# Pair 13 of the second layer's last down product: seven products instead of eight

## The chip, the cores and the metric

The kernel runs on one core of a Trainium2 chip. The time is the device time of one execution in microseconds (us); the figure for a kernel is the median of its runs. The core has a matrix engine (TensorE; PE in the profile, PEld for its weight loads), a vector engine (DVE), a scalar engine (ACT), GpSimd (POOL) and SyncE (SP), whose queue issues the loads of the weights. Each engine works through its own instructions in a fixed order and waits for the others by semaphores. Matmuls accumulate in PSUM, in eight banks of 128 x 512 floats; everything else lies in SBUF.

## The reference

Two layers over 256 tokens of width 2048. The first layer mixes tokens by a convolution module, the second by multi-head latent attention; behind each mixer stands an MLP with a squared ReLU, of inner width 8192, and a final norm ends it all. The change touches the MLP of the second layer alone:

```python
def sq_relu_mlp(h, w1, w2):
    return jnp.square(jax.nn.relu(h @ w1)) @ w2

for layer in range(DEPTH):                  # DEPTH = 2
    ...
    h = rms_norm(x, norm_mlp_g[layer])
    x = x + sq_relu_mlp(h, mlp_w1[layer], mlp_w2[layer])   # w1 2048 x 8192, w2 8192 x 2048
return rms_norm(x, final_norm_g)
```

All values are float32.

## The kernel before

**High and low parts.** A float32 product is made of three matmuls (`mm3`, lines 201 to 205): each operand is split into a high part `hi`, the value rounded by an ACT copy to the matmul's type, and a low part `lo`, the rest, made by a DVE subtraction. For weights this is `upper_half` and `lower_half` (lines 164 to 175; in the profile `hi` at L170 on ACT and `lo` at L174 on DVE). In `mm3` the first matmul (L203) and the second (L204) read the weight's high part, the third (L205) its low part. "A product" is such a group of three, for 128 rows of weights (a row block), 128 tokens and 512 columns.

**The MLP** (`mlp`, lines 609 to 755) goes through the inner width in two halves (`hf`) of 32 row blocks. In each half the up product (lines 640 to 687) comes in eight groups of four row blocks, and leaves the squared ReLU of each group, split, in SBUF. The down product follows: the half's 32 row blocks of `w2`, 256 tokens (T = 2 blocks of 128), 2048 columns.

**Pairs of row blocks.** The down product takes the row blocks in 16 pairs, 2p and 2p + 1. For one pair, both token blocks and a pair of column blocks (2 x 512) it has to make a product of two 2 x 2 block matrices. A plain pair (`Sums.plain`, line 559) makes it by eight products. A mixed pair (`Sums.mixed`, line 546) makes it by seven, in Winograd's form: seven sums and differences of the weights' blocks (`mixed_weights`, line 490) and of the activations' blocks (`mixed_inputs`, line 512), accumulated in four sums `e` and four sums `u` in the eight PSUM banks, which `join` (line 582) puts together and `close` (line 595) adds to the residual `xs`.

The weights of a mixed pair are one load of two row blocks by 1024 columns, and after it, on ACT and DVE: the split of the two blocks of the first 512 columns (b11 and b21), the split of one block of the others (b22), three subtractions in place (L505 of 128 x 1024, L506 and L507 of 128 x 512), the split of t1 and t3, the split of t4 and t2. The splits are L497 on ACT and L498 on DVE, three of 128 x 1024 and one of 128 x 512. A plain pair has two splits of 128 x 1024 (L170, L174) and no subtractions. Where other products came before it, a mixed pair's seven products go in the order b11, b21, b22, t1, t3, t4, t2 (line 555); the fourth is thus the first that needs t1's parts.

**Which pairs are mixed** is the table `MIXED` (line 44): for each layer and half the numbers of the pairs. Three halves have eight, the last half of the second layer has seven, without pair 13, the other pair of group 6. `mixed` (line 637) is the list of groups that have mixed pairs, and their tiles, `sh` and `sl` in the profile, have room for seven blocks of inputs in both pairs either way; `gh` and `gl` are those of plain groups. In the up product, the pairs in `ms` go through `mixed_inputs` (line 679), the others are split by L686 on ACT and L687 on DVE.

**The order in a usual column pair** (lines 708 to 728): HEAD plain pairs first, then the mixed pairs spread among the plain ones, `join` ahead of the last plain pair. This holds for both column pairs of three halves, and for columns 0 to 1023 of the last half.

**The last column pair of the last half** (lines 731 to 754) is another matter. Its columns 1024 to 1535 and 1536 to 2047 are made by `product_A` (line 417) one after the other, with the mixed pairs' work in the first of them, since they feed both. The plain row blocks go in units: each plain group is a unit of four row blocks, and a plain pair of a mixed group is a unit of two, behind the first. A unit is one load, two splits and eight products (four for two blocks). `between` decides how many mixed pairs go behind each unit, in proportion to the row blocks done:

```python
units = [list(range(4 * g, 4 * g + 4)) for g in plain]
units[1:1] = [[2 * p, 2 * p + 1] for p in ps if p // 2 in mixed]
...
def between(n, u, due):
    if n == n2 and u < nu - 1:
        while at_[0] < min(len(ms), -(-len(ms) * sum(map(len, units[: u + 1])) // sum(map(len, units[:-1])))):
            mixed_quad(sums, at_[0])
            at_[0] += 1
    if n == n2 and u == nu - 1:
        sums.join(room)
```

The last block (columns 1536 to 2047) does all but the last three units for both token blocks together (`n_end = 3`); these three it does for the first token block and then for the second, so that the first block's final norm and store go beside the second's products. `before` (line 1907) multiplies the finished columns by the final gain on DVE (L1865).

**Buffers.** Loaded weights (`raw`) have three buffers (line 155), high and low parts (`hi`, `lo`) six each (`WB`). A mixed pair takes four of the six, a plain pair or a unit two. A load is issued when its `raw` buffer has been split; a split can start when the matmuls that read its `hi` or `lo` buffer are done. The instructions' order on each engine is fixed when the kernel is built; it follows the program, with joining steps set in where they fit.

Of the kernel before, what the change touches and what calls it, by code (L numbers as in the profile page):

```python
# [40 lines left out]
PAD_O = 56  # L41
WB = 6
LOOK = WB // 2 - 1
MIXED = {(layer, half): (0, 1, 4, 5, 8, 9, 12) + (13,) * (layer + half < 2) for layer in range(2) for half in range(2)}
N_MIXED = 4
HEAD, TAIL = (2, 1), 2

# [32 lines left out]
def trunk_kernel(  # L80
# [528 lines left out]
    def mlp(layer, ssq, next_gain, finish=None, before=None, beside=None, after_up=None):  # L609

        with ExitStack() as cx:
# [22 lines left out]
            for hf in range(HALVES):  # L634
                last = hf == HALVES - 1
                ms = MIXED[layer, hf]
                mixed = sorted({p // 2 for p in ms})
# [1306 lines left out]
```

## Time and profile before

| what | us |
|---|---|
| runs: median of 3 (lowest to highest) | 1934.27 (1934.19 to 1934.36) |
| profiled execution: first to last instruction | 1932.5 |
| second layer's MLP, up product of the first half | 1241.3 to 1419.1 |
| its down product | 1419.1 to 1582.3 |
| up product of the last half | 1582.3 to 1759.8 |
| down product of the last half, columns 0 to 1023 | 1759.8 to 1842.1 |
| the same, columns 1024 to 1535, with the seven mixed pairs | 1842.1 to 1899.9 |
| the same, columns 1536 to 2047, and the end | 1899.9 to 1932.5 |

The profile is of one execution, and its clock starts with the first instruction; the runs' times hold what lies around it too. The matmuls are pipelined: a row of the timeline gives 0.39 us for one, but they start every 0.227 us, and a wait of TensorE shows as a larger distance between two starts. A row of the busy times by stretch has: the stretch, its length, then for TensorE, its weight loads, DVE, ACT and POOL the busy time and the number of instructions, the granted TensorE clock (1.00 is full speed), the share of time in which the DMA engines were busy, and GB/s. A row of the timeline has the start, the length, the engine, the line, the operation, what is written and read, the shapes and the count of instructions that it merges, and in brackets the engine's idle time before and who ended it. A row of the groups has the count, the busy time and the mean in ns, and behind the second bar the idle time.

### The profile page before, as it was taken

The numbers are of one execution on the slowest core, as the hardware profiler recorded it, in microseconds if no ns is written. First come the engines' busy times: TensorE is split into PE (matmuls) and PEld (weight loads), VectorE is DVE, ScalarE is ACT, GpSimd is POOL, SyncE is SP. The second block draws the span as 40 slices with busy tenths as digits, with TensorE's granted clock in tenths as the row PEclk, the third lists the DMA queues.
The fourth block names the chain that finished last, engine by engine and source line by source line (L and its number), as shares of the span: only waits on it lengthen the run. The fifth ranks groups of instructions, "written<-read, shape, count | busy, mean of one in ns | idle before, by whom it ended". The sixth has DMA issues, their size and how long they took to land.

```text
span 1932.5 us, 28477 instructions
## 1 busy us (share of the span) xinstructions
PE 1921.0 (99%) x10725; PEld 1681.5 (87%) x10725; DVE 1592.2 (82%) x2457; ACT 1095.6 (57%) x1636; POOL 249.0 (13%) x208
## 2 busy tenths in 40 slices
PE   9999999999999999999999999999999999999998
PEld 8999888888888888888898998888888888888887
DVE  7999988877999776799976766877789987678998
ACT  5667755554555545555576655555555554455554
POOL 6999200000010100000001420000000010000000
PEclk9999999999999999999999999999999999999999
DMA  7766456665585866655656545465646776665774
GB/s 230 214 183 189 153 189 206 193 194 177 175 251 194 263 195 187 194 174 196 217 176 175 142 134 192 155 216 186 188 162 225 222 248 212 191 196 175 231 219 150
DMA packets 230427, 375.50 MB, mean 194 GB/s; under 512 B 16392, under 2 KB 107792, under 8 KB 230032
## 3 DMA queue, kind: packets, MB, share of 16 engines
q1 hardware_dynamic: 224640, 363.28, 58.7%
q0 software_dynamic: 4320, 7.87, 2.2%
q10 hardware_dynamic: 1328, 2.52, 0.4%
q8 instruction: 84, 1.38, 0.3%
q14 instruction: 55, 0.45, 0.1%
HBM read 363.68 MB, written 2.10 MB: 189 GB/s over the span
## 4 chain that ended last, share of the span: by engine, by line
PE 97%; DVE 2%; DMA 0%; ACT 0%; issue 0%; ACTq 0%; DVEq 0%
PE acc L655 24%; PE acc L205 15%; PE acc L203 15%; PE acc L204 15%; PE acc L656 13%; PE acc L823 8%; PE acc L1287 2%; DVE sum L910 1%; DMA xs<-in_x 0%; PE acc L1535 0%; PE acc L1566 0%; PE acc L1565 0%; PE acc L1536 0%; PE acc L1564 0%; PE acc L1537 0%; PE tr L267 0%
## 5 line engine op out<-in xcount | busy, mean ns | idle before, releaser
L174 DVE TENSOR_TENSOR lo<-raw,hi 128x1024 fp32r<-128x1024 f32 (+2 forms) x509 | 602.2, 1197 | 232.3 <-ACT hi L170 226.6
L170 ACT ACTIVATE hi<-raw 128x1024 fp32r<-128x1024 f32 (+2 forms) x574 | 583.9, 1036 | 361.1 <-PE acc L655 203.7
L655 PE MATMUL acc<-xt,hi 128*128 128x512 f32 x2048 | 710.6, 390 | 0.0
L656 PE MATMUL acc<-xt,lo 128*128 128x256 f32 x2048 | 577.5, 282 | 0.0
L655 PEld LDWEIGHTS acc<-xt,hi 128*128 128x128 f32 x2048 | 384.3, 188 | 80.7
L656 PEld LDWEIGHTS acc<-xt,lo 128*128 128x128 f32 x2048 | 387.1, 189 | 0.2
L497 ACT ACTIVATE hi<-raw 128x1024 fp32r<-128x1024 f32 x248 | 228.7, 948 | 228.3 <-DVE raw L505 134.0
L498 DVE TENSOR_TENSOR lo<-raw,hi 128x1024 fp32r<-128x1024 f32 x248 | 263.9, 1087 | 27.6 <-ACT hi L497 22.5
L203 PE MATMUL acc<-hi,sh 128*128 128x512 f32 x514 | 200.1, 389 | 0.0
L205 PE MATMUL acc<-lo,sh 128*128 128x512 f32 x514 | 200.1, 389 | 0.0
L203 PE MATMUL acc<-hi,gh 128*128 128x512 f32 (+1 forms) x516 | 200.0, 388 | 0.0
L205 PE MATMUL acc<-lo,gh 128*128 128x512 f32 (+1 forms) x516 | 199.9, 387 | 0.0
L204 PE MATMUL acc<-hi,gl 128*128 128x512 f32 (+1 forms) x516 | 199.9, 387 | 0.0
L823 PE MATMUL acc<-xt,hi 128*128 128x256 f32 x1024 | 180.2, 281 | 0.3 <-ACT b L1106 0.2
L204 PE MATMUL acc<-hi,sl 128*128 128x512 f32 x450 | 175.1, 389 | 0.0
L578 POOL DMA_DIRECT2D xs<-v x30 | 26.5, 994 | 1136.4 <-DVE lo L174 703.2
L910 DVE SCALAR_TENSOR_TENSOR sum<-ub,w_dw,sum 128x256 f32<-128x256 f32 x409 | 164.3, 481 | 3.6 <-ACT sum L880 3.0
L174 POOL TENSOR_TENSOR lo<-raw,hi 128x1024 fp32r<-128x1024 f32 x65 | 155.0, 2410 | 17.3 <-ACT hi L170 17.3
L823 PEld LDWEIGHTS acc<-xt,hi 128*128 128x128 f32 x1024 | 154.8, 188 | 1.1 <-ACT xt L1090 0.6
L823 PE MATMUL acc<-xt,lo 128*128 128x256 f32 x512 | 139.2, 279 | 0.0
L205 PEld LDWEIGHTS acc<-lo,sh 128*128 128x128 f32 x514 | 96.5, 188 | 20.4 <-DVE lo L498 0.3
L204 PEld LDWEIGHTS acc<-hi,gl 128*128 128x128 f32 x516 | 96.9, 188 | 19.9
(314 smaller groups left out, 2531.3 us busy)
## 6 DMA issues: line engine op xcount, KB each, us to landing
raw<-in_mlp_w SPq DMA_DIRECT2D x255, 1024.0 KB, 5.5
raw<-in_conv_w_pw SPq DMA_DIRECT2D x62, 512.0 KB, 5.1
raw<-in_conv_w_pw SPq DMA_DIRECT2D x16, 1024.0 KB, 5.1
raw<-in_mla_w_o SPq DMA_DIRECT2D x16, 1024.0 KB, 5.7
raw<-in_mla_w_kv_up SPq DMA_DIRECT2D x32, 256.0 KB, 3.9
xs<-v POOLq DMA_DIRECT2D x30, 256.0 KB, 7.8
raw<-in_mla_w_in SPq DMA_DIRECT2D x8, 576.0 KB, 3.8
raw<-in_mla_w_in SPq DMA_DIRECT2D x4, 1024.0 KB
```

What stands on the lines that cost most here:

```text
L170: nc.scalar.activation(hi, raw[:, js, :], AF.Copy)
L174: eng.tensor_tensor(lo, raw, hi.bitcast(F32), op=ALU.subtract)
L203: nc.tensor.matmul(ps, sh, mh, start=start, stop=False)
L204: nc.tensor.matmul(ps, sl, mh, start=False, stop=False)
L205: nc.tensor.matmul(ps, sh, ml, start=False, stop=stop)
L497: nc.scalar.activation(hi, src, AF.Copy)
L498: nc.vector.tensor_tensor(lo, src, hi.bitcast(F32), op=ALU.subtract)
L655: nc.tensor.matmul(ps[b], wh[:, bs], xhl(k), start=k == 0, stop=False)
L656: nc.tensor.matmul(ps[b][:, :S], wl[:, bs], xh(k), start=False, stop=k == KC - 1)
L823: nc.tensor.matmul(pss[c][b][:, :S], w[i][:, bs], (xh, xl)[j](k), start=k == i + j == 0, stop=end and k == k0 + nk - 1 and (i, j) == terms ...
L910: nc.vector.scalar_tensor_tensor(out=out, in0=ubs[c][:, w : w + S], scalar=tap(c, w), in1=base, op0=ALU.mult, op1=ALU.add)
L1287: nc.tensor.matmul(ps2[b][t], x_kt(k, t), w[:, bs], start=k == g == i == 0, stop=k == KC - 1 and i == len(group) - 1,)
```

## The change

Pair 13 joins the mixed pairs of the second layer's last half, which then has the same eight as the three other halves. It is one line; `mixed`, `plain`, `units` and the order of the work follow from it.

```diff
-MIXED = {(layer, half): (0, 1, 4, 5, 8, 9, 12) + (13,) * (layer + half < 2) for layer in range(2) for half in range(2)}
+MIXED = {(layer, half): (0, 1, 4, 5, 8, 9, 12, 13) for layer in range(2) for half in range(2)}
```

What follows from it in the last half:

- up product, group 6: the second pair of its inputs goes through `mixed_inputs` instead of L686 and L687;
- columns 0 to 1023: eight mixed and eight plain pairs instead of seven and nine, ordered by the same rule;
- the last column pair: the unit of two row blocks is gone from both column blocks; the units are four of four row blocks, and behind the first three of them `between` puts 3, 3 and 2 mixed pairs, where it put 2, 1, 2 and 2 behind the first four of five. In the last block one unit instead of two goes ahead of the last three.

## The prediction

> **What bounds the kernel now.** First the page's busy times and its chain of waits.
>
> ```profile
> PE 1921.0 (99%) x10725; PEld 1681.5 (87%) x10725; DVE 1592.2 (82%) x2457; ACT 1095.6 (57%) x1636; POOL 249.0 (13%) x208
> ...
> PE 97%; DVE 2%; DMA 0%; ACT 0%; issue 0%; ACTq 0%; DVEq 0%
> ```
>
> Over the span it is TensorE: 97% of the chain. But a share over the span says nothing of the one stage that is changed, so next come the busy times by stretch. The first two rows are the up products of layer 1's two halves, then the first half's down product by column pairs (both with eight pairs), then the last half's columns 0 to 1023, its columns 1024 to 1535 up to the end of the last seven-product pair, one period of that stretch, the rest of the matmuls, and the end.
>
> ```profile
> 1241.00:1419.00 178.00, 178.00 (x1028) 157.68 (x1027) 134.25 (x214) 93.51 (x136) 0.00 (x0) 1.00 0.60 190
> 1582.00:1759.80 177.80, 177.80 (x1027) 157.56 (x1026) 124.51 (x181) 90.06 (x125) 1.78 (x2) 1.00 0.66 205
> 1419.20:1500.70 81.50, 81.50 (x361) 67.49 (x360) 77.24 (x85) 45.65 (x53) 3.51 (x4) 1.00 0.59 195
> 1500.70:1582.20 81.50, 81.50 (x361) 67.47 (x360) 75.49 (x79) 47.03 (x51) 5.26 (x6) 1.00 0.71 223
> 1759.90:1842.10 82.20, 82.20 (x364) 68.08 (x364) 74.62 (x82) 45.26 (x52) 3.50 (x4) 1.00 0.65 214
> 1842.10:1894.50 52.40, 52.40 (x232) 43.36 (x232) 51.02 (x55) 31.16 (x37) 1.75 (x2) 1.00 0.64 197
> 1863.86:1879.65 15.79, 15.79 (x71) 13.06 (x71) 15.50 (x18) 9.08 (x10) 0.00 (x0) 1.00 0.62 198
> 1894.50:1924.70 30.20, 30.20 (x145) 25.34 (x143) 25.51 (x43) 15.29 (x29) 0.00 (x0) 1.00 0.46 157
> 1924.70:1928.70 4.00, 0.03 (x1) 0.00 (x0) 3.13 (x11) 1.42 (x3) 0.00 (x0) 1.00 0.18 62
> 1928.80:1932.50 3.70, 0.00 (x0) 0.00 (x0) 0.00 (x0) 0.00 (x0) 0.00 (x0) 0.50 0.56 203
> ```
>
> Everywhere the matmuls run at one pace, 81.50 us for some 360, with no stall. The reader is to see the DVE column: in the period from 1863.86 it is busy 15.50 of 15.79 us. There DVE is as full as TensorE, and the question is which of the two is ahead. That is read from the timeline: TensorE's matmuls in the last half's second stage (a start of a unit each; L205 is the product that reads a low part),
>
> ```profile
> 1842.14 0.39 PE L203 MATMUL acc<-hi,gh 128*128 128x512 f32 x1
> ...
> 1847.58 0.39 PE L203 MATMUL acc<-hi,sh 128*128 128x512 f32 x1
> ...
> 1884.98 0.39 PE L203 MATMUL acc<-hi,sh 128*128 128x512 f32 x1
> ...
> 1889.74 0.39 PE L203 MATMUL acc<-hi,sh 128*128 128x512 f32 x1
> ...
> 1892.23 0.39 PE L205 MATMUL acc<-lo,sh 128*128 128x512 f32 x1
> ...
> 1913.99 0.39 PE L205 MATMUL acc<-lo,gh 128*128 128x512 f32 x1
> ```
>
> and DVE's instructions that make the low parts for them (start, length, count at the end).
>
> ```profile
> 1843.84 3.63 DVE L498 TENSOR_TENSOR lo<-raw,hi 128x1024 fp32r<-128x1024 f32 x3
> ...
> 1853.14 1.29 DVE L174 TENSOR_TENSOR lo<-raw,hi 128x512 fp32r<-128x512 f32 x2
> ...
> 1859.15 2.52 DVE L498 TENSOR_TENSOR lo<-raw,hi 128x1024 fp32r<-128x1024 f32 x2
> ...
> 1863.86 1.82 DVE L498 TENSOR_TENSOR lo<-raw,hi 128x1024 fp32r<-128x1024 f32 x2
> 1865.59 1.22 DVE L505 TENSOR_TENSOR raw<-raw 128x1024 f32<-128x1024 f32 x1
> ...
> 1872.35 1.22 DVE L505 TENSOR_TENSOR raw<-raw 128x1024 f32<-128x1024 f32 x1
> ...
> 1879.65 1.82 DVE L498 TENSOR_TENSOR lo<-raw,hi 128x1024 fp32r<-128x1024 f32 x2
> ...
> 1890.73 2.52 DVE L498 TENSOR_TENSOR lo<-raw,hi 128x1024 fp32r<-128x1024 f32 x2
> ...
> 1910.18 1.28 DVE L1865 TENSOR_TENSOR xs<-xs,gf 128x512 f32<-128x512 f32 x2
> 1911.43 2.36 DVE L174 TENSOR_TENSOR lo<-raw,hi 128x1024 fp32r<-128x1024 f32 x2
> ```
>
> Prices: a plain unit of four row blocks is 24 matmuls, 1842.14 to 1847.58 = 5.44 us on TensorE, so a product (three matmuls) is 0.68; a seven-product pair is 1884.98 to 1889.74 = 4.76. On DVE such a pair costs 1865.59 to 1872.35 (L505 to the next L505) = 6.76, and a period of two of them and a plain unit 1863.86 to 1879.65 = 15.79, so the unit 15.79 - 13.52 = 2.27. A seven-product pair thus costs DVE 2.00 more than it gives TensorE to do; a plain unit gives back 3.17. A period loses 0.83 (15.79 against 14.96). At the last pair of the stage the lead is nearly used up: t1 and t3's low parts are there at 1890.73 + 1.22 = 1891.95, and the fourth product reads them at 1892.23. The slack is 0.28 us.
>
> **The change, part by part.** *Matmuls.* Pair 13 (row blocks 26 and 27) takes seven products instead of eight in each column pair: 2 x 0.68 = 1.36 us less.
>
> *Its inputs* (`mixed_inputs` in the up product's group 6) replace one ACT and one DVE instruction by three of each and four small sums.
>
> ```profile
> L519 DVE TENSOR_TENSOR sl<-v,sh 128x128 fp32r<-128x128 f32 (+2 forms) x21 | 9.7, 464 | 0.2
> ...
> L687 DVE TENSOR_TENSOR gl<-v,gh 128x512 fp32r<-128x512 f32 x6 | 4.1, 685 | 0.0
> L528 DVE TENSOR_TENSOR v<-v 128x128 f32<-128x128 f32 x7 | 2.0, 284 | 0.0
> ```
>
> DVE: 3 x 0.464 + 4 x 0.284 - 0.685 = 1.84 us more. I take 0: group 7's up product covers it, DVE is busy 124.5 of 177.8 us there, and the first half's up product, with eight pairs, runs 1028 matmuls in 178.0 against 1027 in 177.8. Without that cover it would cost up to 1.84.
>
> *Columns 0 to 1023.* The order becomes that of the three other halves (two plain, two mixed, plain, two, plain, one, plain, two, plain, one, plain, joining, plain). They run it without a stall (81.50 for 361), DVE at 77.24. No cost; 0.68 of the 1.36 is gained here.
>
> *Columns 1024 to 1535, in the last product.* Units were {4 blocks, pair 13, 4, 4, 4} with 2, 1, 2, 2 mixed pairs behind the first four; they become {4, 4, 4, 4} with 3, 3, 2. From the stage's start S, the eighth pair would begin, unstalled, at 3 x 5.44 + 7 x 4.76 = 49.64, and read t1's low part as the seventh does now, 1892.23 - 1889.74 = 2.49 later: S + 52.13. DVE, from the end of the first pair's low parts (call it S + d): two pairs and a unit 15.79, three and a unit 22.55, two more less the last subtraction 13.52 - 1.25 = 12.27; together 50.61. So t1 is late by d + 50.61 - 52.13 = d - 1.52.
>
> For d there are two rows: here now, 1843.84 and two of the three subtractions, some 2.4 us, to 1846.2 = S + 4.1; and the same border in the first half, whose order the changed kernel has up to there.
>
> ```profile
> 1500.73 0.39 PE L203 MATMUL acc<-hi,gh 128*128 128x512 f32 x1
> ...
> 1503.60 2.50 DVE L498 TENSOR_TENSOR lo<-raw,hi 128x1024 fp32r<-128x1024 f32 x2
> ```
>
> That is 1506.10 - 1500.73 = 5.37. The stall lies between 2.6 and 3.85 by these; the second and third pair went slower here (1846.2 to 1859.15 + 2.52 = 1861.67, less the half unit's 1.29, is 14.18 for 13.52), which adds up to 0.7: upper end 4.6. I take 3.85, by the like order. It comes in parts: some at the fifth pair, about 2 at the sixth, the rest at the eighth, each time when a group's last pairs have used up what the plain unit gave. Behind the waiting matmul stands everything on TensorE, so all of it moves the end.
>
> *The tail.* The last block loses pair 13's unit (4 products, 2.72 on TensorE; 1.29 on DVE). From t1's low part of the last mixed pair to the last unit's first low part DVE takes now 1911.43 + 1.22 - 1891.95 = 20.70, then 19.41; TensorE now 1913.99 - 1892.23 = 21.76, then 19.04. Without today's slack the last unit is late by 0.37. It is 0 if the gain multiplications (L1865) now ahead of it go behind it, and 2.3 if the other such block (0.68 + 1.28) also goes ahead. I take 0.37. What comes after the last matmul is unchanged.
>
> *Transfers.* Pair 13's two 512 KB loads of the last stage become one of 1024 KB: same bytes, one issue fewer on SP's queue, no price at 0.64 DMA share.
>
> Sum: -1.36 + 3.85 + 0.37 = **+2.86 us** on the profiled span of 1932.5, so 1935.4. The median of the runs is 1.77 above that span; with the same distance 1934.27 + 2.86 = **1937.1**. Ends of this case: -1.36 + 2.6 + 0 = +1.2 and -1.36 + 3.85 + 2.3 = +4.8, so 1935.5 to 1939.1. A measurement of this kernel can tell about 0.2% (3.87 us) from no change; most of this case is inside it.
>
> A rule of the Trainium skill would have it otherwise. "Perfetto Trace Analysis", Identifying the Most-Contended Engine, says to find the engine of highest occupancy and work on that one first; by whole-span shares that is TensorE (its LDWEIGHTS row too, 87% against DVE's 82%), and taking matmuls from it at DVE's expense would pay, 1932.9 here. The next section of that page allows for regimes in which the contended engine changes, and the period from 1863.86 is such a regime.
>
> **Rivals.** *No stall: faster by the matmuls, 1934.27 - 1.36 = 1932.9.* It needs DVE to be 3.85 us further ahead. For it: the page's chain is TensorE's, and three stages with eight pairs never stall. Against it: these have at most two such pairs in a row and a 5.44 us plain pair for each, while the last stage has eight of them to four units.
>
> *The first pair's weights land late: slower.* At the border ACT waits for the load.
>
> ```profile
> 1497.10 1.58 ACT L497 ACTIVATE hi<-raw 128x1024 fp32r<-128x1024 f32 x2 [2.15 <-DMA raw<-in_mlp_w]
> ...
> 1836.14 1.58 ACT L497 ACTIVATE hi<-raw 128x1024 fp32r<-128x1024 f32 x2 [3.16 <-DMA raw<-in_mlp_w]
> ```
>
> It came 1842.14 - 1836.14 = 6.0 us before S here and 1500.73 - 1497.10 = 3.6 in the first half: 2.4 apart with one program. Another 2.4 later gives d = 7.8, a stall of 6.2 and 1934.27 + 5.3 = 1939.5. It decides by over 0.2% once the load lands later than 2.6 us before S. Against it: the like order landed at 3.6, and DVE's own queue sets d as well.
>
> *The clock falls in a stall: slower.* The rows of the end show 1.00 for 4.0 us after the last matmul and 0.50 behind that. A stall of over 4 us in one piece would leave matmuls at half speed; 4 us of that cost 2 us, so 1937.1 + 2 = 1939.1. My stalls are of 2 us with matmuls between them. "TensorE: Matmul & The Clock Gate", What's actually happening, puts the limit at about 3.4 us of idleness, which the rows of the end agree with in size; by either no stall here is long enough.
>
> **How the numbers follow.** Stalls that outweigh the saved matmuls: 0.70, likeliest 1937.1, own range 1935.5 to 1939.1. No stall: 0.10 (1932.9). Late load: 0.15 (1939.5). Clock: 0.05 (1939.1 or more). Above 1938.1 lie nearly all of the last two and some 0.13 of the first: slower by over 0.2% 0.32. Faster by over 0.2% would need 3.9 us where only 1.36 can be had: 0.02. The rest, 0.66, within. The range 1934.4 to 1939.8 leaves out the stall-free case and half of the late loads.
>
> **What would show it.** Right: matmul starts in the last stage that stand apart by up to 2 us, released by L498's low parts, first at the fifth or sixth mixed pair, most at the third of a group of three; the eighth pair ending 3.5 to 4.5 us later than 49.64 + 4.76 = 54.4 behind the stage's first matmul; DVE without idle from the first mixed pair to the eighth; no stall in columns 0 to 1023, which end 0.68 earlier. Wrong: no such gaps, or gaps in the up product or in columns 0 to 1023; DVE idle for ACT or a load between mixed pairs; a granted clock below 1.00 before the last matmul.

## The result, and the profile after

| kernel | median us (lowest to highest) | runs |
|---|---|---|
| before | 1934.24 (1933.88 to 1935.25) | 16 |
| changed | 1938.0 (1937.36 to 1939.2) | 16 |

The ratio is 1.0019, with a 95% interval of 1.0012 to 1.0026: 3.76 us slower, inside the 0.2% that a measurement can tell from no change, and above zero. The profiled execution's span went from 1932.5 to 1936.2.

First the busy times by stretch of the changed kernel: the last half's up product, its columns 0 to 1023, and the last stage up to the eighth mixed pair (the columns of such a row are explained ahead of the prediction).

```profile
1582.00:1759.50 177.50, 177.50 (x1026) 157.30 (x1025) 125.31 (x186) 90.62 (x127) 1.79 (x2) 1.00 0.65 205
...
1759.90:1841.40 81.50, 81.50 (x361) 67.50 (x360) 76.20 (x84) 45.49 (x52) 3.50 (x4) 1.00 0.63 208
...
1841.40:1899.00 57.60, 54.56 (x233) 42.92 (x233) 56.54 (x62) 32.31 (x37) 1.75 (x2) 1.00 0.64 197
```

The first two stretches run as those of the first half do, without a pause. In the third TensorE is short of work for the first time, and DVE is busy 56.54 of 57.60 us. The waits of the weight loads in the same execution name what was late (the engine and line that waited, on what, us in total, how often, the longest):

```profile
PEld acc L203 <- ACT hi L497: 4.0, 5, 1.1
PEld acc L205 <- DVE lo L498: 2.1, 2, 1.1
```

The kernel before has no such row in this stage. Where they fall is seen in the timeline of TensorE: the stage's first matmul, and then each matmul that waited (the idle time in brackets is after the modelled end of the one before, so it is less than the extra distance between the starts).

```profile
1841.23 0.39 PE L203 MATMUL acc<-hi,gh 128*128 128x512 f32 x1
...
1858.55 0.50 PE L203 MATMUL acc<-hi,sh 128*128 128x512 f32 x1 [0.16 <-ACT hi L497]
...
1859.96 0.50 PE L205 MATMUL acc<-lo,sh 128*128 128x512 f32 x1 [0.68 <-DVE lo L498]
...
1875.76 0.50 PE L205 MATMUL acc<-lo,sh 128*128 128x512 f32 x1 [0.54 <-DVE lo L498]
...
1881.10 0.50 PE L203 MATMUL acc<-hi,sh 128*128 128x512 f32 x1 [0.71 <-ACT hi L497]
...
1882.56 0.50 PE L203 MATMUL acc<-hi,sh 128*128 128x512 f32 x1 [0.26 <-ACT hi L497]
...
1897.19 0.50 PE L203 MATMUL acc<-hi,sh 128*128 128x512 f32 x1 [0.28 <-ACT hi L497]
...
1898.80 0.50 PE L203 MATMUL acc<-hi,sh 128*128 128x512 f32 x1 [0.41 <-ACT hi L497]
```

These are the third, the fifth, the sixth and the eighth mixed pair. ACT's high parts are late because they are made of what DVE's L505 and L507 leave, as ACT's rows of the sixth and the eighth pair show, so both kinds of row point at DVE.

```profile
1879.99 1.06 ACT L497 ACTIVATE hi<-raw 128x1024 fp32r<-128x1024 f32 x1 [2.77 <-DVE raw L505]
1881.44 1.06 ACT L497 ACTIVATE hi<-raw 128x1024 fp32r<-128x1024 f32 x1 [0.39 <-DVE raw L507]
...
1897.69 1.06 ACT L497 ACTIVATE hi<-raw 128x1024 fp32r<-128x1024 f32 x1 [0.55 <-DVE raw L507]
```

The last wait of the stage is for the last of these: t4 and t2's high parts of the eighth pair, ready at 1898.75, and the matmul that reads them starts at 1898.80.

Summed over the matmuls, what their distances exceed 0.227 us by is 4.95 us. Reckoned the other way: from the first to the last matmul of the last half's down product it took 164.61 us before and 168.39 after, 3.78 more, which is -1.36 for the six matmuls and 5.14 of stall.

DVE's timeline of the changed kernel at the stage's border, in the first long run of mixed pairs and at its end:

```profile
1839.66 1.83 DVE L498 TENSOR_TENSOR lo<-raw,hi 128x1024 fp32r<-128x1024 f32 x2 [1.73 <-ACT hi L497]
...
1845.07 3.64 DVE L498 TENSOR_TENSOR lo<-raw,hi 128x1024 fp32r<-128x1024 f32 x3
...
1858.69 2.52 DVE L498 TENSOR_TENSOR lo<-raw,hi 128x1024 fp32r<-128x1024 f32 x2
...
1896.32 0.69 DVE L580 TENSOR_TENSOR xs<-acc,xs 128x512 f32<-128x512 f32 x1
...
1897.51 2.50 DVE L498 TENSOR_TENSOR lo<-raw,hi 128x1024 fp32r<-128x1024 f32 x2
...
1909.86 6.90 DVE L174 TENSOR_TENSOR lo<-raw,hi 128x1024 fp32r<-128x1024 f32 x6
```

Two things are to be seen. The first pair starts late, behind 1.73 us of idleness, and t4 and t2's low parts end at 1847.57, 6.35 us behind the stage's first matmul instead of 4.2. And an addition of the joined sums (L580) slipped into the eighth pair. The last row holds all low parts of the last three units: they went ahead of the gain multiplications, where the last unit's had stood behind half of them. What made the first pair late is in ACT's timeline:

```profile
1838.57 1.58 ACT L497 ACTIVATE hi<-raw 128x1024 fp32r<-128x1024 f32 x2 [3.27 <-DMA raw<-in_mlp_w]
```

ACT waits for the weights until 2.65 us ahead of the stage's first matmul; in the kernel before it was 6.0.

### The profile page after: what moved, and what is told of

Same layout as the page of the kernel before. It is cut to its first block, busy times and chain, and to the rows that moved or that the text cites. A ratio compares the mean times of both kernels' runs of the same rounds, so it can differ in the third digit from the quotient of the medians.

```text
span 1936.2 us, 28481 instructions
## 1 busy us (share of the span) xinstructions
PE 1921.8 (99%) x10719; PEld 1680.6 (87%) x10719; DVE 1601.2 (83%) x2471; ACT 1099.4 (57%) x1640; POOL 249.0 (13%) x208
## 4 chain that ended last, share of the span: by engine, by line
PE 81%; issue 13%; DVE 3%; DMA 1%; ACT 1%; POOL 0%; ACTq 0%; DVEq 0%; POOLq 0%
PE acc L655 18%; PE acc L205 13%; PE acc L203 13%; PE acc L204 13%; PE acc L656 10%; PE acc L823 8%; PE acc L1287 2%; DVE sum L910 1%; DMA xs<-v 1%; DVE lo L498 1%; DMA xs<-in_x 0%; PE acc L1535 0%; PE acc L1565 0%; PE acc L1564 0%; PE acc L1536 0%
## 5 line engine op out<-in xcount | busy, mean ns | idle before, releaser
L170 ACT ACTIVATE hi<-raw 128x1024 fp32r<-128x1024 f32 (+1 forms) x568 | 579.6, 1039 | 353.1 <-PE acc L655 199.8
L497 ACT ACTIVATE hi<-raw 128x1024 fp32r<-128x1024 f32 (+1 forms) x256 | 235.8, 949 | 235.3 <-DVE raw L505 147.4
L498 DVE TENSOR_TENSOR lo<-raw,hi 128x1024 fp32r<-128x1024 f32 (+1 forms) x256 | 272.1, 1088 | 28.2 <-ACT hi L497 22.7
L203 PE MATMUL acc<-hi,sh 128*128 128x512 f32 x512 | 199.9, 390 | 1.8 <-ACT hi L497 1.8
L205 PE MATMUL acc<-lo,sh 128*128 128x512 f32 x512 | 199.0, 390 | 1.2 <-DVE lo L498 1.2
L203 PE MATMUL acc<-hi,gh 128*128 128x512 f32 (+1 forms) x516 | 200.0, 388 | 0.0
L205 PE MATMUL acc<-lo,gh 128*128 128x512 f32 (+1 forms) x516 | 199.9, 387 | 0.0
L203 PEld LDWEIGHTS acc<-hi,sh 128*128 128x128 f32 x512 | 96.1, 188 | 23.7 <-ACT hi L497 4.0
L205 PEld LDWEIGHTS acc<-lo,sh 128*128 128x128 f32 x512 | 96.1, 188 | 22.1 <-DVE lo L498 2.3
```

The source lines that it names most:

```text
L170: nc.scalar.activation(hi, raw[:, js, :], AF.Copy)
L203: nc.tensor.matmul(ps, sh, mh, start=start, stop=False)
L205: nc.tensor.matmul(ps, sh, ml, start=False, stop=stop)
L497: nc.scalar.activation(hi, src, AF.Copy)
L498: nc.vector.tensor_tensor(lo, src, hi.bitcast(F32), op=ALU.subtract)
```

## The experiments

The experiments ask three things: which of the two column pairs costs the time, what makes the first pair late, and whether it is DVE's sum of work or the order that counts. In the diffs, `sums` is the last stage's object unless said.

### One column pair at a time

```diff
  # eight_then_seven: the last stage with seven
  sums = Sums(NNB - 2, False)
+ ms, ps = ms[:-1], sorted([13] + ps)
```

> Columns 0 to 1023 with eight mixed pairs, the last column pair with seven: pair 13 is plain there, and its plain products read blocks of activations that are not theirs. The theory: the end is DVE's lead over TensorE, and the eighth pair in columns 0 to 1023 alone makes the last stage's first pair ready later (6.2 us behind the stage's start instead of 4.1), which seven pairs with 0.28 us of slack can't bear. So one product less saves 0.68, and some 1.9 us of stall come in the last stage: about 1935.5, 1.2 above before. The rival, the part of the prediction that put columns 0 to 1023 at no cost: 1934.2 - 0.7 = 1933.6, no stall.

Measured: 1935.2 us (1934.16 to 1936.11) beside 1934.37, ratio 1.0004 (0.9994 to 1.0013). The profiled execution has a stall of 1.54 us in the last stage, at its fifth and seventh pair, with the first pair ready at 6.46. So an eighth pair in columns 0 to 1023, which itself runs without a pause, uses up in the next stage what it saves. The prediction's "no cost" for it is wrong by that.

```diff
  # seven_then_eight: columns 0 to 1023 with seven
+ every = ms
+ if split_end:
+     ms, ps = ms[:-1], sorted(ps + [13])
  ks = [2 * p for p in ps]
  ...
+ ms, ps = every, [p for p in ps if p != 13]
  sums = Sums(NNB - 2, False)
```

> The mirror: seven mixed pairs in columns 0 to 1023 (pair 13's plain products there read blocks that are not theirs), eight in the last column pair. The theory: the first pair is ready 4.1 us behind the stage's start as in the kernel before, DVE's rate alone makes the eighth pair late by 4.1 - 1.5 = 2.6, and 0.6 for an adding of joined sums that went ahead of the eighth pair: a stall of 3.2, saved 0.7, about 1936.7 (2.5 above before). Rival one, the late load is the whole cause: stall under 1, at most 1934.5. Rival two, the border does not matter: the changed kernel's time and one product more, 1938.7.

Measured: 1937.44 us (1937.06 to 1937.97), ratio 1.0016 (1.0006 to 1.0025). ACT's row at the border shows the weights as early as in the kernel before, 6.05 us ahead of this execution's stage at 1842.60:

```profile
1836.55 1.58 ACT L497 ACTIVATE hi<-raw 128x1024 fp32r<-128x1024 f32 x2 [3.19 <-DMA raw<-in_mlp_w]
```

The stall is 3.49 us, with the first pair ready at 4.88 instead of the 4.1 expected. Part of that is a wait of DVE for one of the additions by DMA to the residual:

```profile
1843.05 0.69 DVE L601 TENSOR_TENSOR xs<-acc,xs 128x512 f32<-128x512 f32 x1 [0.65 <-DMA xs<-v]
```

The eight pairs of the last stage are the larger cause; they need no late load. Rival one falls, and rival two's 1938.7 isn't reached either: the border matters, but less.

### The late load

At the border the DMA engines are full. The busy times by stretch of the changed kernel, and its DMA queues in nearly the same stretch (1827 to 1844):

```profile
1827.00:1843.00 16.00, 16.00 (x72) 13.27 (x71) 12.93 (x15) 7.65 (x10) 3.50 (x4) 1.00 0.96 281
```

```profile
q1 hardware_dynamic: 1241, 3.84, 65.6%
q0 software_dynamic: 505, 0.94, 30.2%
```

The second queue is `put`: columns 0 to 1023 are added to the residual by accumulating DMAs from GpSimd's queue. They move a fifth of the bytes and take a third of the engines' time.

```diff
  # no_adds: for the Sums of columns 0 to 1023 of the last half
  def put(self, t, c, o):
+     if self.quiet:
+         return
```

> The changed kernel without the six additions of columns 0 to 1023 into the residual by DMA from GpSimd's queue (left out, so these columns lack part of their sum). The theory: the weights of the last stage's first pair are late because these additions share the DMA engines, which are full for 15 us there; without them the load lands at least 3 us ahead of what it does now, the first pair is ready at about 4.3 behind the stage's start instead of 6.2, and the stall falls from 5.1 to about 3.2: 1936.1. The rival, the load is late for its own queue or the buffers: 1938.0, unchanged.

Measured: 1935.87 us (1935.53 to 1936.84), ratio 1.0009 (0.9999 to 1.0018). In the profiled execution, whose last stage starts at 1842.48:

```profile
1828.00:1844.00 16.00, 16.00 (x72) 13.28 (x71) 15.40 (x19) 9.10 (x13) 0.00 (x0) 1.00 0.75 264
```

```profile
1837.30 1.58 ACT L497 ACTIVATE hi<-raw 128x1024 fp32r<-128x1024 f32 x2 [1.70 <-PE acc L205]
```

ACT starts 5.2 us ahead of the stage, and the stall is 2.63 us. The row puts the end of ACT's wait down to a matmul, but the load itself landed within 0.1 us of ACT's start here too. The issue of that load, and its time to landing, first in the changed kernel, then without the additions:

```profile
1829.50 0.37 SPq L160 DMA_DIRECT2D raw<-in_mlp_w  x1
DMA to landing us min/median/max: 9.0/9.0/9.0
...
1830.73 0.37 SPq L160 DMA_DIRECT2D raw<-in_mlp_w  x1
DMA to landing us min/median/max: 6.5/6.5/6.5
```

Read in the same way, the load of the first mixed pair behind a border has, in us:

| execution | issued ahead of the stage's first matmul | issue to landing | landed ahead of it |
|---|---|---|---|
| before | 13.3 | 7.2 | 6.1 |
| seven, then eight | 13.3 | 7.1 | 6.2 |
| before, at the first half's border | 11.7 | 7.9 | 3.8 |
| changed | 11.7 | 9.0 | 2.7 |
| eight, then seven | 11.7 | 9.1 | 2.6 |
| no additions | 11.8 | 6.5 | 5.3 |
| additions by DVE (next run) | 11.8 | 6.4 | 5.4 |

So the load is late for two reasons. With eight mixed pairs in the columns ahead of the border it is issued 1.5 us nearer to the stage, and beside the additions, which the kernel before has too, it takes 1.8 us longer than there. That the additions cost it some 2.5 us, 9.0 against 6.5, is shown; the later issue comes with the order of the eight pairs and stays when they are left out. That the DMA engines are full doesn't set the two kernels apart: in the kernel before the same stretch, 1827 to 1843, has a share of 0.96 too.

```diff
  # dve_adds: the same additions by DVE
- sums = Sums(n, not last or split_end)
+ sums = Sums(n, not last)
```

> The changed kernel with the six additions of columns 0 to 1023 made by DVE from PSUM and SBUF instead of by DMA. The theory: the load is early as without additions, but DVE has 6 x 0.6 = 3.6 us more at the border, of which its present 3.0 us of idleness there take most: the first pair is ready some 0.6 later than now, 1938.6 (1937.6 to 1939.4), no gain. The rival, the DMA's contention alone sets the first pair: as without additions, 1935.9.

Measured: 1939.43 us (1939.01 to 1939.76), ratio 1.0028 (1.0017 to 1.0038), just above the theory's range; the rival falls. The load is early, ACT starts 5.3 us ahead, but DVE has the work, and its order got worse by one wait:

```profile
1846.33 0.68 DVE L507 TENSOR_TENSOR raw<-raw 128x512 f32<-128x512 f32 x1
1848.22 2.97 DVE L498 TENSOR_TENSOR lo<-raw,hi 128x1024 fp32r<-128x1024 f32 x3 [1.21 <-ACT hi L497]
```

Here t1 and t3's subtraction was put ahead of L507, and then nothing was left to do while ACT made t4 and t2's high parts: 1.21 us of idleness in each pair so ordered. The first pair is ready at 7.84, the stall 6.25.

### DVE's sum of work, and the order

```diff
  # order_224; the rule is asked ahead of the first unit too, with u = -1
- while at_[0] < min(len(ms), ...):
+ while at_[0] < (2, 4, 8)[u]:
```

> The changed kernel with 2, 2 and 4 mixed pairs behind the first three units of the last stage instead of 3, 3 and 2. The theory: what counts is DVE's sum up to the eighth pair, which stands at the same place behind three units, so the stall is the same in sum though it all falls at the end: 1938.0, within 0.6. The rival, a run of three is what DVE can't keep up with, and a run of four is worse by what a pair overdraws (2.0 us): 1939 to 1940, or, if only the number of such runs counted, below 1937.

Measured: 1946.61 us (1946.45 to 1946.81), ratio 1.0064 (1.0049 to 1.0079). What ran isn't what the expectation speaks of: with u = -1 the table gave 8, and all eight pairs went ahead of the first unit. It is of use as such: eight pairs with no unit between them stall for 13.2 us, near the 7 x 2.0 = 14 that seven more pairs overdraw by the prediction's prices, and the units behind give none of it back. The order that was meant:

```diff
  # order_224b
+ while at_[0] < (0, 2, 4, 8)[u + 1]:
```

> The changed kernel with 2, 2 and 4 mixed pairs behind the first three units, now as meant: the eighth pair stands behind three units as in the changed kernel. The theory (DVE's sum up to the eighth pair against TensorE's): the same stall in sum, all of it in the last run of four: 1938.0, within 0.6. The rival, the length of a run sets it: a run of four is worse by a pair's overdraft, 2.0: 1940.

Measured: 1939.62 us (1939.09 to 1940.4), ratio 1.0028 (1.0018 to 1.0039). The stall is 6.80, not the 5 of the changed kernel: outside the theory's 0.6 and nearer to the rival. But its DVE timeline has another difference than the run of four:

```profile
1868.52 0.68 DVE L507 TENSOR_TENSOR raw<-raw 128x512 f32<-128x512 f32 x1
1870.41 1.23 DVE L498 TENSOR_TENSOR lo<-raw,hi 128x1024 fp32r<-128x1024 f32 x1 [1.21 <-ACT hi L497]
```

The same unlucky order as in the run with DVE's additions came at the last pair of the second group of two, and again in the eighth pair (an idle time of 1.18). These two waits, 2.4 us, are more than the 1.85 by which the stall grew, so the run does not decide between the theory and the rival. It shows that the order that the build gives to DVE's instructions changes with the edit, and can add 1.2 us a time.

```diff
  # late_2222 (the flags that close the accumulations move with it; left out here)
+ while at_[0] < (0, 2, 4, 6)[u + 1]:
  ...
  if n == n2 and u == nu - 1:
+     while at_[0] < len(ms):
+         mixed_quad(sums, at_[0])
+         at_[0] += 1
      sums.join(room)
```

> The changed kernel with 2 mixed pairs behind each of the four units, the last two behind the last unit and the joining after them. The theory: the last pair now has one more unit ahead of it, which gives TensorE 5.44 and costs DVE 2.27, so it is late by 3.2 less; some of that comes back in the last block, where the joined sums are made later: stall about 3.2 for 5.1, 1936.1 (1935.4 to 1936.8). The rival, the order is no lever since DVE has the same work in the stage: 1938.0.

Measured: 1936.37 us (1935.53 to 1937.63), ratio 1.0011 (1.0002 to 1.002); stall 3.24. The order is a lever: 1.6 us less than the changed kernel.

```diff
  # late_no_adds: late_2222, and
  def put(self, t, c, o):
+     if self.quiet:
+         return
```

> The changed kernel with 2 mixed pairs behind each of the four units of the last stage and without the six additions by DMA of columns 0 to 1023 (left out, so these columns lack part of their sum). The theory: the stall falls by the 1.6 of the order and by the 2.1 of the additions: 1934.3 (1933.6 to 1935.0). The rival, both take away the same part of the stall: 1935.9 or more, the better of the two alone.

Measured: 1934.2 us (1933.89 to 1935.82), ratio 1.0001 (0.9992 to 1.0011); stall 1.05. The two gains add up.

```diff
  # eight_seven_late (the same flags left out)
  sums = Sums(NNB - 2, False)
+ ms, ps = ms[:-1], sorted([13] + ps)
  ...
+ while at_[0] < (0, 2, 3, 4, 6)[u + 1]:
  ...
  if n == n2 and u == nu - 1:
+     while at_[0] < len(ms):
+         mixed_quad(sums, at_[0])
+         at_[0] += 1
```

> Eight mixed pairs in columns 0 to 1023, seven in the last column pair (pair 13's plain products there read blocks that are not theirs), with the last stage's mixed pairs put later: 2, 1, 1, 2 behind the first four of its five units and 1 behind the last. The theory: the eighth pair in columns 0 to 1023 costs nothing but lead at the border, and later mixed pairs give more than the 2.3 us of lead back, so the stall goes and the product saved shows: 1933.6 (1933.4 to 1934.2). The rival, the later load costs its 1.5 us of stall in any order: 1935.2.

Measured: 1934.54 us (1933.43 to 1935.64), ratio 1.0002 (0.9993 to 1.0012). The profiled execution, which took 1933.72, has 0.10 us of extra distance left in all and a span of 1931.9, 0.6 below the one before:

```profile
PEld acc L205 <- DVE lo L174: 0.3, 1, 0.3
PEld acc L205 <- DVE lo L501: 0.2, 1, 0.2
```

(The edit moved lines by three: L501 is L498.) So the product saved in columns 0 to 1023 shows when the order gives the lead back, but in the median of ten runs it doesn't; the runs spread over 2.2 us where those of the kernel before spread over 0.8. That the landing of the load, which the profiled executions show anywhere from 6.05 to 2.35 us ahead of the stage, is behind the spread is likely and wasn't shown.

```diff
  # extra_dve: in mixed_weights, for the last stage
  nc.vector.tensor_tensor(low[:, 0, :], low[:, 0, :], low[:, 1, :], op=ALU.subtract)
+ if extra:
+     nc.vector.tensor_tensor(low[:, 0, :], low[:, 0, :], low[:, 0, :], op=ALU.max)
```

> The changed kernel with one more DVE instruction of 128 x 512 in each mixed pair of the last column pair (a maximum of a block with itself, which changes nothing). The theory: DVE bounds from the first pair to the eighth, so 8 times about 0.62, 5.0 us more stall: 1943.0 (1942.4 to 1943.6). The rival, only the load of the first pair and the waits in the first run are behind it: under 2 us more, below 1940.

Measured: 1951.2 us (1949.56 to 1952.59), ratio 1.0087 (1.0071 to 1.0102). The direction is the theory's, the size isn't: 18.1 us of stall instead of 10. DVE's timeline (L509 is the added maximum):

```profile
1861.55 0.68 DVE L509 TENSOR_TENSOR raw<-raw 128x512 f32<-128x512 f32 x1
1863.43 1.23 DVE L498 TENSOR_TENSOR lo<-raw,hi 128x1024 fp32r<-128x1024 f32 x1 [1.21 <-ACT hi L497]
```

The added instruction stands last ahead of ACT's copy of t4 and t2, and in seven of the eight pairs DVE waits some 1.2 us for that copy, 8.4 us in all. Some 2 us more are matmuls at about half rate behind TensorE's last long wait, 11 of them in 4 us:

```profile
1911.00:1915.00 4.00, 4.00 (x11) 3.14 (x12) 4.00 (x5) 3.71 (x4) 0.00 (x0) 0.57 0.38 97
```

As a measure of DVE's bare time the run is spoilt; it shows once more what the DVE to ACT to DVE hand-over costs when nothing covers it. The rival, under 2 us, falls.

```diff
  # pool_b22: for the last stage, eng = nc.gpsimd
- (b22,) = halves(raw[:, 1:2, NB:])
+ (b22,) = halves(raw[:, 1:2, NB:], eng)
```

> The changed kernel with one of a mixed pair's four subtractions for the low parts, that of b22 (128 x 512), on GpSimd instead of DVE, in the last column pair alone. The theory: DVE has 8 x 0.6 = 4.8 us less to do up to the eighth pair, and the stall of 5.1 nearly goes: 1933.3 (1932.9 to 1934.6), a little faster than the kernel before. The rival: GpSimd takes at least 1.2 us for one and the subtraction L506 in place has to wait for it, so half of the gain or more is lost: above 1935.5; or GpSimd slows DVE, then DVE's L498 and L505 take longer than 1.22.

Measured: 1942.72 us (1942.09 to 1942.95), ratio 1.0043 (1.003 to 1.0055). The groups of DVE and of GpSimd in the last stage (each behind the kernel's own line), first the changed kernel's L505, then the same of this run and GpSimd's subtraction:

```profile
L505 DVE TENSOR_TENSOR raw<-raw 128x1024 f32<-128x1024 f32 x7 | 8.5, 1220 | 0.0
```

```profile
L505 DVE TENSOR_TENSOR raw<-raw 128x1024 f32<-128x1024 f32 x6 | 13.5, 2244 | 0.2
...
L498 POOL TENSOR_TENSOR lo<-raw,hi 128x512 fp32r<-128x512 f32 x6 | 12.7, 2110 | 30.4 <-ACT hi L497 30.4
```

DVE saves 0.6 us a pair and pays 1.02, since L505 beside GpSimd's subtraction takes 2.24 instead of 1.22; with a little idleness a pair takes DVE 7.32 (L505 to L505) instead of 6.76. Moving this subtraction to GpSimd makes it worse. The rival's second branch, that GpSimd slows DVE, is what happened.

## Why the prediction was right, and where it was off

**The mechanism** was right in the main: DVE falls behind with the weights of the last stage's eight mixed pairs, and the stall outweighs the 1.36 us of matmuls saved. 1938.0 lies in the range, 0.9 above the 1937.1 named. The operand was only partly the one named: the prediction had TensorE wait for L498's low parts, and five of the seven waits (4.0 of 6.1 us) were for ACT's high parts of what DVE's subtractions in place leave. Of the signs named, the eighth pair ends at 1900.76, 59.5 behind the stage's first matmul and 5.1 later than 54.4 (3.5 to 4.5 had been named); columns 0 to 1023 end 0.68 earlier; and between the first mixed pair and the eighth DVE isn't idle.

**The sum.** Predicted -1.36 + 3.85 + 0.37 = +2.86; measured -1.36 + 5.14 = +3.78 between the first and last matmul. These terms were off:

- d, the time at which the first pair is ready, was taken as 5.37 from the like border of the first half and was 6.35. The prediction had the mechanism as a rival (a late load) with a chance of 0.15, and took the first half's 3.6 us of lead for it; it was 2.65. At the first half's border the load was issued just as late, 11.7 us ahead, but took 7.9 us instead of 9.0. That the additions by DMA lengthen it is shown; why by 1.1 us more here stays open. In six other executions with this order and the additions it took 8.3 to 9.3 us, in the three without them 6.4 to 6.5. That is 0.98 of the difference.
- An addition of joined sums (L580, 0.6 on DVE) inside the eighth pair was not in the chain.
- The matmuls' order in the eighth pair wasn't the one of line 555 that the sum took over from the seventh pair. The build put four high-part matmuls of t1 and t3 and the first of t4 (L203 at 1897.19 to L203 at 1898.80) ahead of the first low-part one (L205 at 1899.14), so t1's low part is read later, and what is waited for last is t4's high part: ready at 1898.75, 57.52 behind the stage's first matmul, for a matmul that unstalled would start 13 matmuls into the pair, at 49.64 + 2.95 = 52.59. That is 4.93 late, where t1's low part by the prediction's order (1897.51 + 1.22 = 1898.73, so 57.50 against 52.13) would have been 5.37: about 0.4 less.
- The tail cost 0, the lower of the two ends given, because its low parts went ahead of the gain multiplications.

3.85 + 0.98 + 0.6 - 0.4 = 5.0, against 4.95 summed over the distances and 5.14 between first and last matmul. That the miss is only 0.9 us is in part luck: the order and the tail took back some of what the late load and the addition cost. The rule behind it, a stall of d - 1.5 and a little, can be read against the experiments, for all those with 3, 3 and 2 mixed pairs on the last stage's units:

| run | weights' split starts ahead of the stage | d | stall |
|---|---|---|---|
| no additions | 5.2 | 3.82 | 2.63 |
| seven, then eight | 6.05 | 4.88 | 3.49 |
| changed | 2.65 | 6.35 | 4.95 |
| additions by DVE | 5.3 | 7.84 | 6.25 |

(d is the end of t4 and t2's low parts of the first pair; both from the starts in the timeline.) The stall is d less 1.2 to 1.6 in all four.

**Where it showed up.** Predicted: first at the fifth or sixth pair. It was the third. By the prediction's own prices t1's low part of the third pair is late by d + 13.52 - 1.25 - (5.44 + 2 x 4.76 + 2.49) = d - 5.18, which is 0.19 even with its 5.37; it hadn't worked this out. With 6.35 it is 1.2, and the distances there exceed 0.227 by 1.4 in all. **The inputs of pair 13** cost nothing: 1026 matmuls in 177.5 us. **Columns 0 to 1023** ran without a pause as predicted, but the step "no cost" failed at its border: alone with seven behind it, they gave a stall of 1.54 us.

**The rivals.** No stall: refuted by the first fence of waits. The late load: part of it, not the whole (with an early load 2.63 and 3.49 us of stall remain). The prediction put the point at which it decides at 2.6 us ahead of the stage, and here it landed 2.7 ahead. The clock: in the changed kernel 1.00 throughout the last stage; but its reason, that only a wait of over 4 us in one piece would do it, was wrong (below).

**A version that beats both** was not found. At most 1.36 us can be had, and the two orders that give most of the stall back come out at 1934.2 and 1934.5, with parts left out or misread, beside 1934.1 for the kernel before.

## What to carry to other kernels

A scheme that trades matmuls for vector work is priced in the stage where it goes, by the lead of the one engine over the other: read how long ahead of its use the last operand is ready (0.28 us here), and what one more exchange adds on either side (here a mixed pair for the unit of two row blocks: 6.76 - 1.29 = 5.5 us of DVE's time against 4.76 - 2.72 = 2.0 of TensorE's). Such a lead is inherited across a border between stages, so an edit that is free in its own stage can be paid in the next. And an engine's order is part of the price: a hand-over between two engines that had been covered by other work costs its full 1.2 us when the order shifts.

## What the hardware showed that was not expected

**The granted clock can fall after short waits.** In the run with GpSimd's subtractions, TensorE waited twice within 1.5 us, and behind that its matmuls start 0.43 us apart. Its timeline, and the granted clock of that stretch (0.72, the third number from the right of the row, left of DMA share and GB/s):

```profile
1860.43 0.50 PE L203 MATMUL acc<-hi,sh 128*128 128x512 f32 x1 [1.22 <-ACT hi L497]
...
1861.91 0.79 PE L205 MATMUL acc<-lo,sh 128*128 128x512 f32 x1 [0.75 <-DVE lo L498]
1862.50 0.63 PE L203 MATMUL acc<-hi,sh 128*128 128x512 f32 x1
1862.93 0.63 PE L204 MATMUL acc<-hi,sl 128*128 128x512 f32 x1
```

```profile
1860.00:1866.00 6.00, 4.82 (x13) 3.58 (x14) 5.90 (x6) 4.79 (x6) 0.67 (x1) 0.72 0.32 100
```

The run with the added DVE instruction has the same, in the busy times of 1883 to 1888 a clock of 0.53:

```profile
1883.00:1888.00 5.00, 5.00 (x13) 3.94 (x13) 4.93 (x6) 2.19 (x3) 0.00 (x0) 0.53 0.56 176
```

No single distance between starts there is over 2.2 us, far under the 4 us that the end of the kernel before had suggested. Nor do such waits always do it: the run with GpSimd's subtractions has the same two waits again, 1.20 and 0.75 us of idleness, at 1884.66 and 1886.15, and the clock stays at 1.00.

```profile
1883.00:1889.00 6.00, 4.05 (x17) 2.70 (x16) 5.79 (x7) 4.98 (x6) 0.00 (x0) 1.00 0.33 105
```

The Trainium skill, "TensorE: Matmul & The Clock Gate", What's actually happening, says that the gate watches how busy TensorE was in a free-running window of about 3.4 us, and calls for an idle one; here the clock fell to about half though no wait was that long, so the measurement goes further than the page. A free-running window would explain that one pair of waits does it and the other doesn't; where the windows lie isn't shown.

**GpSimd and DVE hold each other up.** A subtraction of 128 x 1024 on DVE went from 1.22 to 2.24 us beside one of GpSimd's, which itself takes 2.11 us for 128 x 512. In one pair, DVE's low parts, GpSimd's subtraction and DVE's L505:

```profile
1870.22 3.66 DVE L498 TENSOR_TENSOR lo<-raw,hi 128x1024 fp32r<-128x1024 f32 x3
...
1873.03 2.00 POOL L498 TENSOR_TENSOR lo<-raw,hi 128x512 fp32r<-128x512 f32 x1 [5.33 <-ACT hi L497]
...
1873.91 2.20 DVE L505 TENSOR_TENSOR raw<-raw 128x1024 f32<-128x1024 f32 x1
```

DVE's low parts kept their 1.22 each and ended at 1873.88, with GpSimd's already begun; GpSimd's ended 1.15 behind that, at 1875.03, and L505 1.08 behind that, at 1876.11. The rows read as if the two took turns, the later one waiting for the earlier to end; no run tests this, and GpSimd's times in a profile are rough. "GPSIMD Engine Reference", Specifications, of the Trainium skill has the cause, shared SBUF interfaces that contend where a DVE instruction has two SBUF inputs, without a price; these rows agree that there is such contention.

**Accumulating DMAs are dear.** In the border's 17 us, 0.94 MB of them took 30.2% of the engines' time and 3.84 MB of plain loads 65.6%: 1.9 times as much for a byte. The load beside them took 9.0 us to land, and 6.5 without them.
